# A mixture-of-experts decoder layer: two fixed units for the experts' outputs, and another look-ahead for the weights

## The chip, the cores and the metric

The kernel runs on one core of a Trainium2 chip. The metric is the device time of one execution in microseconds (us); the median of three runs is given, and beside it one execution that the hardware profiler recorded.

## The reference, cut to what matters

One decoder layer: a spatial gating MLP and a differential attention side by side, a cross-attention into 256 memory tokens, and a mixture of 32 experts, each token using two of them. The change lies in the experts:

```python
def hierarchical_moe(h, w_rg, b_rg, w_re, b_re, w_gate, w_up, w_down):
    ...                                  # routing: 1024 tokens, 2 experts each
    def expert_rows(args):               # xb: 128 rows of 1024, for one expert
        xb, e = args
        g = xb @ w_gate[e]               # 1024 x 512
        u = xb @ w_up[e]                 # 1024 x 512
        return (jax.nn.silu(g) * u) @ w_down[e]      # 512 x 1024
    y_rows = lax.map(expert_rows, (x_rows, block_expert)).reshape(P, D)
    ...
    out = jnp.einsum('nk,nkd->nd', wts.astype(y.dtype), y)
```

## The kernel before, in words

The last 600 us are the 32 experts, one after the other, each on one block of 128 rows. The input rows of an expert are gathered (POOL, an indirect DMA) into one of three buffers `xg`. `x_t` transposes them on TensorE (eight matmuls with the identity into the PSUM tile `px`) and splits them into a high part `xth` (a cast on ACT) and a low part `xtl` (a subtraction on DVE). `gate_up` multiplies by the gate and the up weights: 8 weight tiles, 48 matmuls of 128x512 into two PSUM tiles `pgu`, each product being three matmuls (high by high, high by low, low by high: `mm3`). ACT and DVE then form `hh` (DVE's step, L1424, ends it). `h_t` transposes `hh` (four matmuls into `pt`) and splits it into `ht`; `down` multiplies by 4 further weight tiles (24 matmuls into `py`). ACT scales `py` into a unit `y` in SBUF (L1450), and POOL issues a scatter that adds the rows of `y` to the tokens in DRAM (`x2d`, L1451). Each scatter waits for the landing of the one before.

`down(e-1)` is called after `gate_up(e)` and `x_t(e+1)`, and `h_t(e)` after that. The order of the instructions of POOL and SP is that of the code. The order of TensorE, ACT and DVE is that of the code for the first two experts and from the 31st on; between, a scheduler that works when the program is built puts it together, by what it believes is ready when. The order is then fixed: at run time each engine waits in that order.

Every weight tile (512 KB, `raw`) is loaded by SP, cast by ACT (`whi`, L280) and its rest formed by DVE (`wlo`, L281). `raw`, `whi`, `wlo`, `xth`, `xtl`, `ht` and `y` all take units of 128x1024 out of one pool of 45 (`unit`, tag "u"): a tile that is taken must wait until what last used its unit has let go of it. `pump` issues loads up to `ahead["load"]` tiles beyond the one in use: 31 tiles for experts 0 to 15, 10 from expert 16 on, 20 for the last. PSUM has one tag "pd" with two buffers for `px` and `py` alike, and one with four for `pgu` and `pt`.

After expert 30's scatter has landed, SP loads the 1024 tokens back (`xf`, eight loads, L1513), POOL gathers the rows of the last expert (L1515), and squares, norms, scaling and stores follow.

Of the kernel before, what the change touches and what calls it, by code (L numbers as in the profile page):

```python
# [19 lines left out]
D = 1024  # L20
KT = 8
H = 512
NE = 32
# [13 lines left out]
AL = 1  # L37
MD = 4.0
NX = 3
LA = 30  # L40
LE = 31
LD = 2
LS = 3
PF = 3
RM = {mybir.EngineType.DVE, mybir.EngineType.PE, mybir.EngineType.Activation}
PK = 12
LF = 10
EF = 16
JT = 0
ED = 1  # L50
KQ = lambda nc: nc.gpsimd
# [58 lines left out]
def tile_layer(tc, a, out):  # L110
# [12 lines left out]
    def unit(name, shape, dt=F32):  # L123
        return up.tile(shape, dt, name=name, tag="u", bufs=NU)
# [7 lines left out]
    def ps2(name="pd"):  # L132
        return psum.tile([128, 1024], F32, name=name, tag="pd", bufs=2)

    def mm3(o, sh, sl, mh, ml, start, stop):
        mm(o, sh, mh, start=start, stop=False)  # L136
        mm(o, sh, ml, start=False, stop=False)  # L137
        mm(o, sl, mh, start=False, stop=stop)  # L138
# [41 lines left out]
    def row(t, ap, n):  # L180
        nc.gpsimd.dma_start(t, bass.AP(tensor=ap.tensor, offset=ap.offset, ap=[[0, 128], [1, n]]))
# [81 lines left out]
    ahead = {"load": 3, "split": 1}  # L263
# [21 lines left out]
    def take():  # L285

        j = ptr["use"]
        ptr["use"] += 1
        pump()
        k = plan[j][1]  # L290
        return [t.rearrange("p (k c) -> p k c", k=k) for t in parts.pop(j)]
# [752 lines left out]
    def gather(e):  # L1044
        x = xg[e % NX]
        nc.gpsimd.indirect_dma_start(out=x, out_offset=None, in_=td[:, :],
                                     in_offset=bass.IndirectOffsetOnAxis(ap=idx[:, e:e + 1], axis=0),
                                     bounds_check=S - 1, oob_is_err=False)
# [333 lines left out]

    ahead["load"], ahead["split"] = LA, LS

    xts = {}
    def x_t(e):
        x = xg[e % NX]
        if e == 0:
            xh, xl = unit("xth", [128, D], F32R), unit("xtl", [128, D], F32R)
            for i in range(2):  # L1390
                p = ps1("px")
                cs = slice(512 * i, 512 * i + 512)
                for k in range(4):
                    nc.tensor.transpose(p[:, k * 128:(k + 1) * 128], x[:, (4 * i + k) * 128:(4 * i + k + 1) * 128],
                                        ident)
                split(xh[:, cs], xl[:, cs], p)
            xts[e] = (xh, xl)
            return
        px = ps2("px")
        for k in range(KT):  # L1400
            nc.tensor.transpose(px[:, k * 128:(k + 1) * 128], x[:, k * 128:(k + 1) * 128], ident)
        xh, xl = unit("xth", [128, D], F32R), unit("xtl", [128, D], F32R)
        split(xh, xl, px)
        xts[e] = (xh, xl)

    hts = {}

    def gate_up(e, between=None):
        xh, xl = xts.pop(e)
        gu = []  # L1410
        for w in range(2):
            p = ps1("pgu")
            for q in range(4):
                wh, wl = take()
                for k2 in range(2):
                    k = 2 * q + k2
                    ks = slice(k * 128, (k + 1) * 128)
                    mm3(p, xh[:, ks], xl[:, ks], wh[:, k2], wl[:, k2], k == 0, k == KT - 1)
            gu.append(p)
            if w == 0 and between:  # L1420
                between()
        hh = half("hh")
        nc.scalar.activation(hh, gu[0], AF.Silu, scale=tab[:, 1, e:e + 1])
        nc.vector.scalar_tensor_tensor(hh, gu[1], tab[:, 1, e:e + 1], hh, op0=OP.mult, op1=OP.mult)  # L1424
        hts[e] = hh

    def h_t(e):
        hh = hts[e]
        pt = ps1("pt")
        for k in range(4):  # L1430
            nc.tensor.transpose(pt[:, k * 128:(k + 1) * 128], hh[:, k * 128:(k + 1) * 128], ident)
        x = unit("ht", [128, 2, H], F32R)
        split(x[:, 0], x[:, 1], pt)
        hts[e] = x

    def down(e, between=None):
        x = hts.pop(e)
        py = ps2("py")
        for k in range(4):
            wh, wl = take()  # L1440
            ks = slice(k * 128, (k + 1) * 128)
            for c in range(2):
                cs = slice(c * 512, (c + 1) * 512)
                mm3(py[:, cs], x[:, 0, ks], x[:, 1, ks], wh[:, 0, cs], wl[:, 0, cs], k == 0, k == 3)
            if k == 1 and between:
                between()
        if e == NE - 1:
            return py
        y = unit("y", [128, D])
        nc.scalar.activation(y, py, AF.Copy, scale=tab[:, 0, e:e + 1])  # L1450
        nc.gpsimd.indirect_dma_start(out=x2d[:, :], out_offset=bass.IndirectOffsetOnAxis(ap=idx[:, e:e + 1], axis=0),  # L1451
                                     in_=y, in_offset=None, bounds_check=S - 1, oob_is_err=False,
                                     compute_op=OP.add)
# [11 lines left out]
    def count_blocks():  # L1465

        pc = ps1()
        for t in range(8):
            mm(pc[:, :NE], oneb, Mb[t // 4][:, 3 + t % 4], start=(t == 0), stop=(t == 7))
        nc.vector.tensor_scalar(nb, pc[:, :NE], 128.0, None, op0=OP.is_gt)  # L1470
        for j in range(2, 8):
            nc.vector.tensor_scalar(t1, pc[:, :NE], 128.0 * j, None, op0=OP.is_gt)
            nc.vector.tensor_add(nb, nb, t1)
        nc.vector.tensor_reduce(nov[:, 0:1], nb, axis=AX.X, op=OP.add)
        nc.vector.tensor_copy(novi, nov[:, 0:1])
    for e in range(NE):
        ahead["load"] = LF if e >= NE - EF else max(LE, LA - LD * e)
        gate_up(e, between=(lambda: h_t(0)) if e == 1 else None)
        if e + 1 < NE:
            x_t(e + 1)  # L1480
        if e + 1 + NX < NE:
            gather(e + 1 + NX)
        if e == NE - 2:
            last = tc.manual_schedule(engines=RM)
            last.__enter__()

            down(e - 1, between=lambda: h_t(NE - 2))
            break
        if e:
            down(e - 1)  # L1490
        if e:
            h_t(e)
        if e == 1:
            man.__exit__(None, None, None)
            count_blocks()
        if e == 4:
            with tc.manual_schedule(engines=RM):
                nr = nc.values_load(novi[0:1, 0:1], min_val=0, max_val=NOV - 1,
                                    skip_runtime_bounds_check_because="2048 assignments leave at most 15 further blocks")
        if e == PK:  # L1500
            gfin = unit("gfin", [128, D])
            row(gfin, a["norm_final"], D)


    e = NE - 1

    ahead["load"], ahead["split"] = 20, 5
    down(e - 1)
    st = op.tile([128, 2, 9], F32, name="rfin")
    xf = [unit("xf", [128, D]) for _ in range(8)]  # L1510
# [75 lines left out]
    with tc.If(nr > 0):  # L1586
# [63 lines left out]
        with tc.For_i(0, nr, 1) as b:  # L1650
# [41 lines left out]
            y = unit("oy", [128, D])  # L1692
# [51 lines left out]
def _build(arrays):  # L1744
    import numpy as np
    import concourse.bacc as bacc
    nc = bacc.Bacc("TRN2", target_bir_lowering=False, num_devices=1)
    a = {n[3:]: nc.dram_tensor(n, v.shape, mybir.dt.from_np(v.dtype), kind="ExternalInput").ap()
         for n, v in arrays.items()}
    out = nc.dram_tensor("out_0_dram", (S, D), mybir.dt.from_np(np.dtype("float32")), kind="ExternalOutput").ap()  # L1750
    with tile.TileContext(nc, schedule_with_timeline_sim=True) as tc:
        tile_layer(tc, a, out)
    return nc
# [8 lines left out]
```

## Time and profile before

| | |
|---|---|
| median of 3 runs | 1395.27 us (1391.04 to 1400.35) |
| the profiled execution | 1395.21 us |
| its span | 1393.3 us (1.9 us lie outside) |
| TensorE (PE) busy | 1321.9 us, 95% |
| VectorE (DVE) busy | 1002.0 us, 72% |
| ScalarE (ACT) busy | 836.1 us, 60% |

The span runs from the first instruction to the last. Of the busy share of TensorE one subtracts what the clock does to it: a matmul of 128x512 follows the one before after 0.23 us at full clock. Times below are counted from the span's start.

### The profile page before, as it was taken

The numbers are of one execution on the slowest core, as the hardware profiler recorded it, in microseconds if no ns is written. First come the engines' busy times: TensorE is split into PE (matmuls) and PEld (weight loads), VectorE is DVE, ScalarE is ACT, GpSimd is POOL, SyncE is SP. The second block draws the span as 40 slices with busy tenths as digits, with TensorE's granted clock in tenths as the row PEclk, the third lists the DMA queues.
The fourth block names the chain that finished last, engine by engine and source line by source line (L and its number), as shares of the span: only waits on it lengthen the run. The fifth ranks groups of instructions, "written<-read, shape, count | busy, mean of one in ns | idle before, by whom it ended". The sixth has DMA issues, their size and how long they took to land. (4 is left out here: it accounts for less than half of the span.)

```text
span 1393.3 us, 20524 instructions
## 1 busy us (share of the span) xinstructions
PE 1321.9 (95%) x7424; PEld 1145.1 (82%) x7424; DVE 1002.0 (72%) x1564; ACT 836.1 (60%) x1139; POOL 253.3 (18%) x284
## 2 busy tenths in 40 slices
PE   6999999999999999999998799999989999999992
PEld 4999998989887889999887688888778888888871
DVE  5787694677856444433455798999979999999985
ACT  6554553455555543333232588888868888888874
POOL 2421110311112321112112121111111111111010
PEclk9999999999999999999998899999999999999995
DMA  7640211311275664013699799999999699999986
GB/s 277 194 139 2 60 61 46 91 55 30 84 255 200 201 240 162 19 44 104 227 332 329 256 336 375 362 357 356 353 368 350 217 376 376 367 355 370 376 293 260
DMA packets 103225, 322.39 MB, mean 231 GB/s; under 512 B 15747, under 2 KB 23971, under 8 KB 103120
## 3 DMA queue, kind: packets, MB, share of 16 engines
q1 hardware_dynamic: 76896, 272.14, 53.2%
q0 software_dynamic: 17776, 40.51, 10.2%
q10 hardware_dynamic: 8448, 8.39, 1.8%
q8 instruction: 59, 0.97, 0.3%
q14 instruction: 46, 0.38, 0.1%
HBM read 287.10 MB, written 46.66 MB: 240 GB/s over the span
## 5 line engine op out<-in xcount | busy, mean ns | idle before, releaser
L281 DVE TENSOR_TENSOR wlo<-raw,whi 128x1024 fp32r<-128x1024 f32 (+1 forms) x469 | 557.3, 1227 | 76.4 <-ACT whi L280 68.8
L280 ACT CAST whi<-raw 128x1024 fp32r<-128x1024 f32 (+1 forms) x469 | 472.8, 1050 | 65.5 <-DVE wlo L281 10.8
L136 PE MATMUL pgu<-whi,xth 128*128 128x512 f32 x512 | 198.6, 396 | 4.4 <-ACT whi L280 3.3
L137 PE MATMUL pgu<-wlo,xth 128*128 128x512 f32 x512 | 201.1, 393 | 1.0 <-DVE wlo L281 1.0
L138 PE MATMUL pgu<-whi,xtl 128*128 128x512 f32 x512 | 200.4, 391 | 0.5 <-DVE xtl L142 0.5
L1451 POOL DMA_INDIRECT x2d<-y,idx x31 | 50.9, 1641 | 450.5 <-ACT y L1450 412.1
L136 PEld LDWEIGHTS pgu<-whi,xth 128*128 128x128 f32 x512 | 96.7, 189 | 26.0 <-ACT whi L280 5.2
L137 PEld LDWEIGHTS pgu<-wlo,xth 128*128 128x128 f32 x512 | 96.8, 189 | 22.8 <-DVE wlo L281 2.2
L138 PEld LDWEIGHTS pgu<-whi,xtl 128*128 128x128 f32 x512 | 96.7, 189 | 20.9 <-DVE xtl L142 1.2
L137 PE MATMUL py<-wlo,ht 128*128 128x512 f32 x256 | 104.0, 406 | 1.8 <-DVE wlo L281 1.8
L136 PE MATMUL py<-whi,ht 128*128 128x512 f32 x256 | 102.6, 401 | 0.7 <-ACT ht L141 0.7
L138 PE MATMUL py<-whi,ht 128*128 128x512 f32 x256 | 100.9, 394 | 0.0
L645 ACT ACTIVATE p<-p,stt 128x128 f32<-128x128 f32 (+7 forms) x64 | 49.7, 776 | 50.0 <-DVE stt L644 45.6
L137 PE MATMUL pp<-wlo,hTh 128*128 128x256 f32 x256 | 72.7, 284 | 1.3 <-DVE wlo L281 1.3
L136 PE MATMUL pp<-whi,hTh 128*128 128x256 f32 x256 | 73.1, 286 | 0.2 <-ACT whi L280 0.2
L136 PE MATMUL pp<-whi,h2h 128*128 128x256 f32 x256 | 73.1, 285 | 0.0
L137 PE MATMUL pp<-wlo,h2h 128*128 128x256 f32 x256 | 72.5, 283 | 0.0
L138 PE MATMUL pp<-whi,hTl 128*128 128x256 f32 x256 | 72.5, 283 | 0.0
L138 PE MATMUL pp<-whi,h2l 128*128 128x256 f32 x256 | 72.5, 283 | 0.0
L136 PE MATMUL pp<-hTh,whi 128*128 128x512 f32 x160 | 64.3, 402 | 0.4 <-ACT ot L697 0.4
L137 PE MATMUL pp<-hTl,whi 128*128 128x512 f32 x160 | 63.7, 398 | 0.0
L138 PE MATMUL pp<-hTh,wlo 128*128 128x512 f32 x160 | 63.4, 396 | 0.0
(365 smaller groups left out, 2941.2 us busy)
## 6 DMA issues: line engine op xcount, KB each, us to landing
raw<-in_w_gate SPq DMA_DIRECT2D x128, 512.0 KB, 10.6
raw<-in_w_up SPq DMA_DIRECT2D x128, 512.0 KB, 12.5
raw<-in_w_down SPq DMA_DIRECT2D x128, 512.0 KB, 11.2
raw<-in_w_in SPq DMA_DIRECT2D x19, 512.0 KB, 3.7
raw<-in_w_kv_mem SPq DMA_DIRECT2D x16, 512.0 KB, 5.9
raw<-vwd SPq DMA_DIRECT2D x16, 512.0 KB, 4.2
raw<-in_w_q_memT SPq DMA_DIRECT2D x8, 512.0 KB, 5.2
raw<-in_w_out SPq DMA_DIRECT2D x8, 512.0 KB, 5.3
```

Source lines behind the costliest of these rows:

```text
L136: mm(o, sh, mh, start=start, stop=False)
L137: mm(o, sh, ml, start=False, stop=False)
L138: mm(o, sl, mh, start=False, stop=stop)
L280: nc.scalar.copy(hi[:, c], raw[:, c])
L281: ahead.get("lo", nc.vector).tensor_tensor(lo[:, c], raw[:, c], hi[:, c].bitcast(F32), op=OP.subtract)
L645: nc.scalar.activation(pe[:, :nk], pe[:, :nk], AF.Exp, bias=stt[:, 2 + m:3 + m], scale=slopes[hd], accum_out=stt[:, 4 + m:5 + m])
L1451: nc.gpsimd.indirect_dma_start(out=x2d[:, :], out_offset=bass.IndirectOffsetOnAxis(ap=idx[:, e:e + 1], axis=0), in_=y, in_offset=None, bou ...
```

## The change

The outputs of the experts no longer take a unit of the pool each time. Two units are taken once, ahead of the loop, and expert e uses the unit `ys[e % 2]`. The look-ahead of the loads is 29 tiles up to expert 11 and 27 from expert 12 (`PK`) on; the numbers LD, LF and EF with which it fell to 10 from expert 16 are gone. The last expert keeps its 20.

```diff
-LA = 30
-LE = 31
-LD = 2
+LA = 29
+LE = 29
...
-LF = 10
-EF = 16
...
     hts = {}
+    ys = [unit("y", [128, D]) for _ in range(2)]
...
-        y = unit("y", [128, D])
+
+        y = ys[e % 2]
         nc.scalar.activation(y, py, AF.Copy, scale=tab[:, 0, e:e + 1])
...
     for e in range(NE):
-        ahead["load"] = LF if e >= NE - EF else max(LE, LA - LD * e)
+        ahead["load"] = LE if e < PK else LE - 2
```

The lines of the changed kernel stand two or three lower than before (`y` is L1449 there, `pt` L1429, `px` L1398, `whi` L277). Since the pool's units go round in another way, the scheduler finds other moments at which things are ready, and the order on TensorE, ACT and DVE differs from about expert 11 on. Three places follow. "waits X" names the engine or DMA queue whose semaphore the instruction waits for.

TensorE at expert 24, from the last matmuls of its `pgu` (which end ahead of the excerpt of before, 13 matmuls of `py` above its `pt`); before:

```order
L138 MATMUL py<-whi,ht 128x512
L136 MATMUL py<-whi,ht 128x512 [waits Activation_49]
L1431 MATMUL pt<-ident,hh 128x128 [waits DVE_49]
L1431 MATMUL pt<-ident,hh 128x128 x3
L137 MATMUL py<-wlo,ht 128x512 [waits DVE_49]
L138 MATMUL py<-whi,ht 128x512
L136 MATMUL py<-whi,ht 128x512
L137 MATMUL py<-wlo,ht 128x512
L138 MATMUL py<-whi,ht 128x512
L1401 MATMUL px<-ident,xg 128x128 [waits DMASW6_49,DVE_49]
L1401 MATMUL px<-ident,xg 128x128 x7
L136 MATMUL py<-whi,ht 128x512 [waits Activation_49]
```

And now:

```order
L133 MATMUL pgu<-whi,xth 128x512
L134 MATMUL pgu<-wlo,xth 128x512
L135 MATMUL pgu<-whi,xtl 128x512
L1429 MATMUL pt<-ident,hh 128x128 [waits DVE_49]
L1429 MATMUL pt<-ident,hh 128x128 x3
L1398 MATMUL px<-ident,xg 128x128 [waits DMASW4_49,Activation_49]
L1398 MATMUL px<-ident,xg 128x128 x7
L133 MATMUL py<-whi,ht 128x512 [waits DVE_49]
L134 MATMUL py<-wlo,ht 128x512
L135 MATMUL py<-whi,ht 128x512
```

The transposes `pt`, which wait for `hh` of the same expert, moved from among the matmuls of `py` to right behind the last matmul of `pgu`, `px` comes right behind them, and the first matmul of `py` now waits for DVE: for `xtl`, since `py` takes the PSUM buffer that `px` had.

DVE at the same expert, around `hh`; before:

```order
L281 TENSOR_TENSOR wlo<-raw,whi 128x1024 [waits DMAHW3_49,DVE_49,Activation_49]
L1424 SCALAR_TENSOR_TENSOR hh<-pgu,tab,hh 128x512 [waits PE_49]
L281 TENSOR_TENSOR wlo<-raw,whi 128x1024 [waits DMAHW4_49,DVE_49,Activation_49]
L142 TENSOR_TENSOR xtl<-px,xth 128x1024 [waits Activation_49]
L281 TENSOR_TENSOR wlo<-raw,whi 128x1024 [waits DMAHW5_49,Activation_49]
```

And now:

```order
L278 TENSOR_TENSOR wlo<-raw,whi 128x1024 [waits DMAHW4_49,PE_49,Activation_49]
L1422 SCALAR_TENSOR_TENSOR hh<-pgu,tab,hh 128x512 [waits PE_49]
L139 TENSOR_TENSOR xtl<-px,xth 128x1024 [waits DVE_49,Activation_49]
L278 TENSOR_TENSOR wlo<-raw,whi 128x1024 [waits DMAHW5_49,Activation_49]
L278 TENSOR_TENSOR wlo<-raw,whi 128x1024 [waits DMAHW6_49,DVE_49,Activation_49]
```

Here `xtl` stands next to `hh`, one `wlo` earlier than before.

ACT where the weights of expert 13 are cast; before:

```order
L1450 ACTIVATE y<-py,tab 128x1024 [waits PE_49]
L141 CAST ht<-pt 128x512 [waits DVE_49]
L280 CAST whi<-raw 128x1024 [waits DMAHW1_49,DVE_49]
L280 CAST whi<-raw 128x1024 [waits DMAHW2_49,PE_49]
L280 CAST whi<-raw 128x1024 [waits DMAHW3_49,DMASW0_49]
L280 CAST whi<-raw 128x1024 [waits DMAHW4_49,DMASW2_49,Activation_49]
L1423 ACTIVATE hh<-pgu,tab 128x512 [waits PE_49]
```

And now:

```order
L138 CAST ht<-pt 128x512 [waits DVE_49,PE_49]
L1449 ACTIVATE y<-py,tab 128x1024 [waits DMASW4_49]
L1449 ACTIVATE y<-py,tab 128x1024 [waits DMASW6_49,PE_49]
L277 CAST whi<-raw 128x1024 [waits DMAHW1_49,DVE_49]
L277 CAST whi<-raw 128x1024 [waits DMAHW2_49]
L277 CAST whi<-raw 128x1024 [waits DMAHW3_49,PE_49]
L277 CAST whi<-raw 128x1024 [waits DMAHW4_49,PE_49]
L277 CAST whi<-raw 128x1024 [waits DMAHW5_49,DVE_49]
```

The waits of the casts for POOL's queue of DMAs (DMASW, the scatters) are gone; in their place the writes of `y` wait for the scatter of two experts before, and two of them stand side by side here. The same happens at the end: the writes of `y` of experts 28 and 29 stand next to each other, where before sixteen other instructions lay between. Experts 25 and 29 have the same order as 24; at 26, 27 and 28 `px` comes right behind `pgu`, then `pt`, then `py`; at 30 `px`, then `py`. At 11, 22 and 23 `pt` comes right behind `pgu` and `py` behind it, whose first matmul waits for `xtl` too; at 12 it waits for `xtl` alone, which stands ahead of `hh` there. Experts 13 to 21 have no such wait behind `pgu`.

## Rows read from the trace of the kernel before

**Rows 1.** The page: busy time, share of the span, instructions.

```profile
PE   1321.9 (95%) x7424; PEld 1145.1 (82%) x7424; DVE 1002.0 (72%) x1564; ACT 836.1 (60%) x1139; POOL 253.3 (18%) x284
```

**Rows 2.** Windows: length, busy PE, PEld, DVE, ACT, POOL, clock, DMA share, GB/s.

```profile
1074.00:1098.00 24.00, 24.00 (x114) 19.96 (x113) 22.34 (x21) 20.81 (x24) 5.50 (x4) 1.00 0.43 136
1098.00:1250.00 152.00, 152.00 (x726) 126.68 (x725) 140.67 (x130) 124.34 (x137) 23.95 (x16) 1.00 1.00 368
1250.00:1340.00 90.00, 89.66 (x420) 73.74 (x419) 83.18 (x77) 75.75 (x83) 11.95 (x8) 1.00 1.01 372
```

**Rows 3.** Timeline of POOL, experts 11 to 14: start, duration, instruction, idle before.

```profile
1011.84 1.58 POOL L1451 DMA_INDIRECT x2d<-y,idx  x1 [14.47 <-DMA raw<-in_w_down]
...
1037.05 1.61 POOL L1451 DMA_INDIRECT x2d<-y,idx  x1 [21.63 <-ACT y L1450]
...
1055.90 1.60 POOL L1451 DMA_INDIRECT x2d<-y,idx  x1 [15.55 <-ACT y L1450]
...
1073.66 1.58 POOL L1451 DMA_INDIRECT x2d<-y,idx  x1 [14.43 <-ACT y L1450]
```

**Rows 4.** Timeline of ACT, the late cast.

```profile
1020.70 1.04 ACT L280 CAST whi<-raw 128x1024 fp32r<-128x1024 f32 x1 [4.34 <-issue]
```

**Rows 5.** Timeline of PE, the same place.

```profile
1021.80 0.54 PE L136 MATMUL pgu<-whi,xth 128*128 128x512 f32 x1 [2.16 <-ACT whi L280]
```

**Rows 6.** Window behind it, same columns as rows 2.

```profile
1022.20:1028.90 6.70, 5.98 (x15) 4.60 (x15) 5.05 (x5) 4.85 (x6) 0.00 (x0) 0.50 0.90 349
```

**Rows 7.** Waits of ACT, 1250 to 1350: total, times, longest.

```profile
ACT whi L280 <- DMA raw<-in_w_down: 7.9, 7, 2.2
```

**Rows 8.** Timeline of PE in an expert without waits.

```profile
1153.29 0.39 PE L138 MATMUL pgu<-whi,xtl 128*128 128x512 f32 x1
...
1156.24 0.60 PE L1431 MATMUL pt<-ident,hh 128*128 128x128 f32 x4
1156.59 0.48 PE L137 MATMUL py<-wlo,ht 128*128 128x512 f32 x1
...
1158.07 1.04 PE L1401 MATMUL px<-ident,xg 128*128 128x128 f32 x8
1158.86 0.48 PE L137 MATMUL py<-wlo,ht 128*128 128x512 f32 x1
```

**Rows 9.** Timeline of DVE, the same expert.

```profile
1153.71 0.75 DVE L1424 SCALAR_TENSOR_TENSOR hh<-pgu,tab,hh 128x512 f32<-128x512 f32 x1 [0.27 <-PE pgu L138]
1154.38 1.22 DVE L281 TENSOR_TENSOR wlo<-raw,whi 128x1024 fp32r<-128x1024 f32 x1
```

**Rows 10.** Timeline of all engines, end of expert 0, where `px` follows `pgu`.

```profile
790.12 0.39 PE L138 MATMUL pgu<-whi,xtl 128*128 128x512 f32 x1
...
790.35 1.03 PE L1401 MATMUL px<-ident,xg 128*128 128x128 f32 x8
...
791.42 1.01 ACT L141 CAST xth<-px 128x1024 fp32r<-128x1024 f32 x1 [0.54 <-PE px L1401]
...
792.47 1.23 DVE L142 TENSOR_TENSOR xtl<-px,xth 128x1024 fp32r<-128x1024 f32 x1 [0.80 <-ACT xth L141]
...
793.75 0.50 PE L138 MATMUL pgu<-whi,xtl 128*128 128x512 f32 x1 [0.53 <-DVE xtl L142]
```

**Rows 11.** Timeline of all engines, last scatter and last expert.

```profile
1350.60 2.48 POOL L1451 DMA_INDIRECT x2d<-y,idx  x1 [9.54 <-ACT whi L280]
...
1356.64 0.75 DVE L1424 SCALAR_TENSOR_TENSOR hh<-pgu,tab,hh 128x512 f32<-128x512 f32 x1
...
1357.44 1.12 PE L1431 MATMUL pt<-ident,hh 128*128 128x128 f32 x4 [2.88 <-DVE hh L1424]
1358.12 2.61 SPq L1513 DMA_DIRECT2D xf<-x2d  x5
...
1359.82 0.63 PE L137 MATMUL py<-wlo,ht 128*128 128x512 f32 x1
```

**Rows 12.** Timeline of PE, the last matmul of `pgu` of expert 30.

```profile
1330.54 0.39 PE L138 MATMUL pgu<-whi,xtl 128*128 128x512 f32 x1
```

## The prediction

> **What bounds the kernel now.** I start with the page: TensorE is busy for 95% of the span [rows 1], so I look for what stops it, stage by stage, and then for what the change puts in its way. The windows of the expert stage come next. From 1098 to 1250 TensorE has no idle time at all (152.00 of 152.00), at full clock [rows 2]. DVE is busy for 140.67 of those 152 us, 93%, and the DMA engines for all of it [rows 2]. TensorE sets the pace, but DVE and the DMA have little to give: a few microseconds lost on TensorE can't be won back later, since its matmuls already follow each other at their own pitch (0.23 us, from the last `pgu` at 790.12 to `px` at 790.35 [rows 10]).
>
> The timeline of POOL shows the pace and the one hole in it. The scatters start at 1011.84, 1037.05, 1055.90 and 1073.66 [rows 3]: 25.2, 18.85, 17.8. The regular period is 17.7. So 25.2 + 18.85 − 35.4 = 8.65 us are lost at expert 13. The timeline of ACT names the cause: a weight cast starts at 1020.70 after 4.34 us of idling put down to "issue" [rows 4], and the order of ACT has this cast wait for a scatter's queue. The scatter issued at 1011.84 lands 8.9 us later, at 1020.7. The cast's unit was the `y` that this scatter still read. TensorE stands for 2.16 us [rows 5] and then runs at a granted clock of 0.50, the 1.2 GHz level, for 6.7 us [rows 6], which costs half of that, 3.35; the rest are shorter gaps around it.
>
> The loads are the second thing that could bound. The look-ahead falls from 31 tiles to 10 at expert 16, and from 1074 to 1098 the DMA idles more than half of the time, 0.43 [rows 2]. After that it works without a break and still, from 1250 to 1350, casts wait for a load of `down` seven times, 7.9 us [rows 7]. TensorE feels little of that: 0.34 of 90 us [rows 2], and about 0.5 as its share of the last scatters' spacing.
>
> **The change, part by part.** *The `y` units.* No weight tile takes over a unit that a scatter reads, so the waits at expert 13 go: −8.65 us. What takes their place is the wait of `y` itself for the scatter of two experts before; 35.4 us lie between, against a landing of 8.9, so it costs nothing where the writes of `y` keep their spacing.
>
> *The look-ahead.* 27 instead of 10 over the second half: there is no pause of the loads. The pause cost 24 us at (1 − 0.43), 13.7 us of DMA time. Against it stand four tiles less than 31 (2.1 MB at 368 GB/s, 5.7 us). The loads of the second half come about 8 us earlier, and the 0.5 us of starved casts go: −0.5.
>
> *The order.* This is the largest term. Behind the last matmul of `pgu` (start S) TensorE used to have 13 matmuls of `py` that needed nothing new, and `pt` came 2.95 us later, at 1156.24 after 1153.29 [rows 8], when `hh` was long done. In ten experts, and at expert 30, the new order puts there something that has yet to be made. The steps from rows: `hh` starts at S + 0.42 (1153.71) and DVE takes the next at S + 1.09 (1154.38) [rows 9]; from the start of `hh` to `pt` 0.80 (1356.64 to 1357.44 [rows 11]); `pt` occupies TensorE for 0.35, `px` for 0.79 [rows 8]; from the start of `px` over `xth` and `xtl` to the matmul that waits for `xtl` 3.40 (790.35 to 793.75), and from the start of `xtl` alone 1.28 (792.47 to 793.75) [rows 10]. Then:
> - Experts 24, 25 and 29 (`pt`, `px`, `py`): `pt` at S + 0.42 + 0.80 = S + 1.22, `px` at S + 1.57, `py` at S + 1.57 + 3.40 = S + 4.97. Without a wait `py` would start at S + 0.23 + 0.35 + 0.79 = S + 1.37. Loss 3.6 each, 10.8.
> - Experts 26, 27 and 28 (`px`, `pt`, `py`): `px` at S + 0.23, `py` at S + 3.63, `pt` lies in between. Loss 3.63 − 1.37 = 2.26 each, 6.8.
> - Expert 23 (`pt`, `py` behind an `xtl` that follows `hh`): `xtl` at S + 1.09, `py` at S + 2.37, against S + 0.58. Loss 1.8. At 11 and 22 the order is the same, but the `wlo` ahead of `hh` may start late, as its unit comes free only with the last tiles; I add 0.85 and 0.65 of at most one `wlo` (1.13 by pitch) as estimates: 2.65 and 2.45. At 12 `xtl` stands ahead of `hh` behind a `wlo` of the same sort, an estimate of 0.9. Together 7.8.
> Sum 25.4 us. What could hide them is `py` not being tied to `px`: it takes the PSUM buffer that `px` of the next expert has just used, and with another it could start at once. In the built order the wait on DVE is there. Bounds: 0 if `xtl` is early for a reason that I don't see; 31 if half of the ten find one more `wlo` of DVE (1.13) in the way.
>
> *Expert 30 and the tail.* `px` and then `py` behind `pgu`: 3.63 − 0.23 − 0.79 = 2.6 on TensorE. On POOL more is lost. The writes of `y` of experts 28 and 29 now stand side by side, late, and that of 27 not far ahead, near the end of expert 30's `pgu`; so four scatters follow, each behind the other's landing. The last scatter of before took 7.5 us until the loads of `xf` (1350.60 to 1358.12 [rows 11]), with few loads beside it. Four times that from S + 1.5 put the `xf` loads at S + 31.5, instead of 1358.12 − 1330.54 [rows 12] = 27.6 or, since at S the new order has some four matmuls fewer behind it, 26.7. I take 5 us, the 2.6 of TensorE lying beside them. Bounds: 2.6, if the writes come earlier; 17, if each of the three spacings is like the one before the last scatter (9.54 of idling [rows 11] and the 1.9 of the scatter ahead, 11.4; 3 × 3.9 more).
>
> *The clock.* Each stall of 2.16 us [rows 5] and of 2.88 us [rows 11] was followed by matmuls at half clock (0.63 a matmul [rows 11] in place of 0.39 [rows 8]); no shorter one in the expert stage was. Seven of the new idle stretches come near, by the steps above and with `pt` and `px` breaking up the longer waits: 3.40 − 0.79 less the transposes that still run, about 2.4, at 24, 25, 29 and 30, and about 2 at 26 to 28. I take one and a half falls at 3.35 us, 5 us; bounds 0 and seven falls, 23.
>
> The Trainium skill, "TensorE: Matmul & The Clock Gate", section "Loop structure matters more than you think", has the clock fall with long waits for DMA and not with a copy by DVE out of PSUM between groups; the new waits are for such a copy. By it the clock term would be 0 and the time 1416.5. Rows 11 speak against it: the 2.88 us there were a wait for DVE, and half clock followed.
>
> Sum against the profiled execution of 1395.2, the same as the median within 0.1: 1395.2 − 8.65 − 0.5 + 25.4 + 5 + 5 = **1421.5 us**. I say 1421.
>
> **The rivals.**
> - *The new waits are hidden; only the gain is left.* The mechanism is that `xtl` and `hh` of the next experts are ready before TensorE asks, because DVE, which was delayed at expert 13 before, runs ahead. It decides from the point at which `xtl` of an expert is done before S + 1.4. For it: DVE idles 7% in rows 2, and experts 13 to 21 have no such wait. Against it: `hh` needs the last `pgu`, which no engine can bring forward, and `px` stands behind `pgu` on TensorE's own queue. Time: 1395.2 − 8.65 − 0.5 = 1386, and 1381 if the tail gains what it was forecast to lose. Not slower, and mostly within 1%.
> - *The clock doesn't fall* (the rule above): 1416.5.
> - *The clock falls at each of the seven and the scatters land late*: four falls instead of one and a half are 8.4 more, 1430; all seven and 5 more in the tail 1444.
> - *The loads starve TensorE.* Twelve loads and a gather and a scatter, 14 × 0.524 MB, take 17.1 us (the loads alone at 368 GB/s) to 19.9 an expert against 17.7. Over seven experts at most 2.2 each: 15, so 1386 + 15 = 1401, if the new waits were hidden. With the new waits TensorE is slower than the loads and nothing is added. Against it: the loads come 8 us earlier than before.
>
> **How the numbers follow.** The forecast with a clock loss of 2 to 8 us (1418 to 1425, and wider by its order term) 0.50; without a clock loss 0.20; clock and scatters high 0.12; waits hidden 0.15; starved with waits hidden 0.03. The likeliest is 1421. The range leaves out the hidden waits (0.18 with the starved ones) and little above: its low end is 1403, about half of the new waits and of the tail (1395.2 − 9.15 + 15.2 = 1401) and no clock loss; its high end is 1434, the forecast with the order's upper bound (+6) and two more falls of the clock (+6.7). Within 1% is about what a measurement of this kernel can tell from no change. Faster by over 1% (below 1381.3): 0.05, a third of the hidden waits. Within 1%: 0.17, the rest of them, the starved case and 0.04 of waits half hidden. Slower by over 1% (above 1409.2): 0.78.
>
> **What the changed profile would show.** Right: scatters at even spacing around expert 13 and no cast with 4.3 us of "issue"; idle time on PE <-DVE `xtl` and `hh` of some 3.6 us an expert at 24, 25 and 29, and 2.3 at 26 to 28, with scatter spacings of about 20 to 21 us there; four scatters in a row some 7.5 to 9 us apart ahead of the `xf` loads; DMA with no pause, but below its full share at the end. Wrong: spacings of 17.7 throughout (the first rival), casts idle for loads (the fourth), or a window of experts 24 to 29 with the clock at 1.00 (the second). The forecast fails most easily if `xtl` runs earlier than `px` by way of a buffer swap that I misread, or by the clock.

## The result, and the profile after

The changed kernel takes 1419.34 us (median of 4 runs, 1414.86 to 1423.43) against 1396.24 of the kernel before (4 runs): a ratio of 1.0162, 95% interval 1.0144 to 1.018. It is slower by 23.1 us. The profiled execution was the slowest of its four, 1423.43 us with a span of 1421.7, so the two profiles differ by 28.4 us. The runs differ in the clock alone, as far as they show: span times mean clock is 1379.0 in the profiled one (1421.7 × 0.970) and 1380.6 in the fastest (1413.1 × 0.977).

The page of the changed kernel, busy time, share and instructions:

```profile
PE   1328.6 (93%) x7424; PEld 1150.1 (81%) x7424; DVE 1000.7 (70%) x1564; ACT 839.9 (59%) x1139; POOL 264.2 (19%) x284
```

TensorE's work is the same (7424 matmuls, as in [rows 1]); its share fell by two points. Where it waits stands in the waits of PE of the changed kernel from 975 to 1375 (engine, line, waited for: us in total, times, longest):

```profile
PE py L133 <- DVE xtl L139: 15.6, 11, 2.4
PE pt L1429 <- DVE hh L1422: 7.8, 8, 1.7
PE py L133 <- ACT y L1449: 0.8, 1, 0.8
```

These are the waits that the prediction read off the built order, eleven of `py` for `xtl` and eight of `pt` for `hh`. The kernel before has neither at experts 11 to 30. The timeline of PE at expert 24, and behind it at 25, shows how they lie (start, duration, instruction, idle before):

```profile
1222.88 0.66 PE L1429 MATMUL pt<-ident,hh 128*128 128x128 f32 x4 [0.85 <-DVE hh L1422]
...
1226.77 0.50 PE L133 MATMUL py<-whi,ht 128*128 128x512 f32 x1 [2.36 <-DVE xtl L139]
```

```profile
1244.27 0.66 PE L1429 MATMUL pt<-ident,hh 128*128 128x128 f32 x4 [0.85 <-DVE hh L1422]
1244.76 1.04 PE L1398 MATMUL px<-ident,xg 128*128 128x128 f32 x8
1248.16 0.50 PE L133 MATMUL py<-whi,ht 128*128 128x512 f32 x1 [2.36 <-DVE xtl L139]
...
1249.65 0.62 PE L133 MATMUL py<-whi,ht 128*128 128x512 f32 x1
```

From the start of `px` (1244.76) to the matmul of `py` (1248.16) 3.40 us pass, to the hundredth what [rows 10] had at the end of expert 0. At 1249.65 the matmul takes 0.62: the clock has fallen. It falls after five of the eight waits of experts 23 to 30, and not after those of 11, 12 and 22. The windows behind the waits of 24 (no fall), 25, 26, 27 (none), 28, 29 and 30, columns as in rows 2 (the clock is the third number from the end):

```profile
1226.70:1231.00 4.30, 4.23 (x18) 3.49 (x19) 3.65 (x5) 2.76 (x4) 0.00 (x0) 1.00 1.03 343
...
1248.00:1254.00 6.00, 5.84 (x19) 4.67 (x20) 4.17 (x5) 2.87 (x4) 0.00 (x0) 0.72 1.02 376
...
1269.60:1276.00 6.40, 6.35 (x21) 5.07 (x22) 4.08 (x4) 3.21 (x4) 0.00 (x0) 0.73 1.02 371
1291.00:1298.00 7.00, 6.89 (x30) 5.73 (x31) 5.76 (x7) 4.69 (x6) 0.00 (x0) 1.00 1.03 390
1310.90:1318.00 7.10, 7.03 (x24) 5.66 (x25) 5.04 (x6) 4.26 (x5) 0.00 (x0) 0.76 0.99 332
1333.90:1341.00 7.10, 7.09 (x24) 5.66 (x25) 5.23 (x5) 4.22 (x5) 0.00 (x0) 0.76 0.66 185
1355.40:1360.00 4.60, 4.60 (x14) 3.67 (x15) 2.21 (x2) 0.58 (x1) 0.00 (x0) 0.63 0.11 21
```

Length times (1 − clock) is the time lost: 6.0 × 0.28 = 1.68, then 1.73, 1.70, 1.70 and 1.70, 8.5 us in all. The clock itself is at half for about 3.4 us each time.

The tail, from the timelines of POOL and SP, the last four scatters and the loads of `xf`:

```profile
1350.85 1.60 POOL L1450 DMA_INDIRECT x2d<-y,idx  x1 [20.63 <-ACT y L1449]
1364.24 1.59 POOL L1450 DMA_INDIRECT x2d<-y,idx  x1 [11.79 <-ACT y L1449]
1370.98 2.16 POOL L1450 DMA_INDIRECT x2d<-y,idx  x1 [5.15 <-ACT whi L277]
1378.75 2.34 POOL L1450 DMA_INDIRECT x2d<-y,idx  x1 [5.61 <-DMA x2d<-y,idx]
```

```profile
1385.60 4.80 SPq L1512 DMA_DIRECT2D xf<-x2d  x8
```

The last three scatters stand 6.7 and 7.8 us apart and the loads come 6.9 behind; in [rows 11] it was 7.5. The first of the four stands 13.4 us ahead of the second, which waited for the write of its `y`.

Where the 28.4 us are shows in the start of the last matmul of `pgu` of each expert (S of the prediction), taken from the timelines of PE, with the distance from one to the next. The regular distance is 17.69.

| expert | before | its step | after | its step | after − before |
|---|---|---|---|---|---|
| 0 | 790.12 | | 792.10 | | +1.98 |
| 10 | 966.41 | 17.69 | 967.16 | 17.69 | +0.75 |
| 11 | 984.71 | 18.29 | 984.62 | 17.46 | −0.09 |
| 12 | 1003.04 | 18.33 | 1005.06 | 20.44 | +2.02 |
| 13 | 1027.92 | 24.88 | 1023.84 | 18.78 | −4.08 |
| 15 | 1064.85 | 18.74 | 1059.40 | 17.66 | −5.45 |
| 22 | 1188.43 | 17.69 | 1182.82 | 17.69 | −5.61 |
| 23 | 1206.12 | 17.69 | 1202.97 | 20.15 | −3.15 |
| 24 | 1223.81 | 17.69 | 1221.64 | 18.67 | −2.17 |
| 25 | 1241.49 | 17.69 | 1243.04 | 21.39 | +1.55 |
| 26 | 1259.18 | 17.69 | 1266.02 | 22.99 | +6.84 |
| 27 | 1276.87 | 17.69 | 1287.48 | 21.46 | +10.61 |
| 28 | 1294.55 | 17.69 | 1307.34 | 19.86 | +12.79 |
| 29 | 1312.85 | 18.30 | 1328.78 | 21.44 | +15.93 |
| 30 | 1330.54 | 17.69 | 1351.77 | 22.99 | +21.23 |
| 31 | 1354.15 | 23.62 | 1380.25 | 28.48 | +26.10 |
| end of span | 1393.3 | | 1421.7 | | +28.4 |

The loss at expert 13 is gone, 3.8 us come in at 12 and 13 (the stalls behind 11 and 12), nothing happens until 22, and from there every expert costs 1 to 5 us more. The step to 24 is the shortest of these because its matmuls have no `px` among them (0.79 us of work in [rows 8]); that `px` stands in the step from 30 to 31, where the kernel before has none.

### The profile page after: what moved, and what is told of

Same layout as the page of the kernel before. It is cut to its first block, busy times and chain, and to the rows that moved or that the text cites. A ratio compares the mean times of both kernels' runs of the same rounds, so it can differ in the third digit from the quotient of the medians.

```text
span 1421.7 us, 20488 instructions
## 1 busy us (share of the span) xinstructions
PE 1328.6 (93%) x7424; PEld 1150.1 (81%) x7424; DVE 1000.7 (70%) x1564; ACT 839.9 (59%) x1139; POOL 264.2 (19%) x284
## 5 line engine op out<-in xcount | busy, mean ns | idle before, releaser
L277 ACT CAST whi<-raw 128x1024 fp32r<-128x1024 f32 (+1 forms) x469 | 474.0, 1049 | 75.2 <-PE py L134 19.7
L133 PE MATMUL py<-whi,ht 128*128 128x512 f32 x256 | 105.5, 412 | 17.1 <-DVE xtl L139 15.6
L135 PE MATMUL py<-whi,ht 128*128 128x512 f32 x256 | 103.0, 402 | 0.0
L133 PEld LDWEIGHTS py<-whi,ht 128*128 128x128 f32 x256 | 49.9, 195 | 30.8 <-DVE xtl L139 17.6
L1043 POOL DMA_INDIRECT xg<-td,idx x32 | 54.0, 1689 | 53.8 <-DVE wsel L1167 17.6
```

The lines of the kernel that those rows point to most:

```text
L277: nc.scalar.copy(hi[:, c], raw[:, c])
```

## The experiments

Two theories stood against each other and a third beside them. A: the time lies in what TensorE finds behind `pgu`, by the order that the scheduler builds. B: the shorter look-ahead costs by itself, through loads that come late. C: the wait of `y` for its scatter costs by itself. All ratios are against the kernel before, run on the same chip.

**The units alone.**

```diff
 # the kernel before, look-ahead 31 and 10 kept
+    ys = [unit("y", [128, D]) for _ in range(2)]
...
-        y = unit("y", [128, D])
+        y = ys[e % 2]
```

> The kernel before with the two fixed units for y alone; the look-ahead stays 31 tiles, and 10 from expert 16 on. Theory A (the loss is the order behind pgu, which only the two parts of the change together bring): the built order has pt among the matmuls of py at every expert and no py that waits for xtl, and no cast waits for a scatter any more, so only the gain is left: 1395 - 9 to 10 = 1386 us, faster than before; no idle stretch of PE over 1 us in the experts, no half clock there. Rival B (the shorter look-ahead itself costs): 1386 too. Rival C (the wait of y for the scatter of two experts before holds ACT up): 1405 to 1420.

1412.92 us, ratio 1.0124 (1.0096 to 1.0152): a miss for A as it was put. In the built order of TensorE `pt` indeed stays among the matmuls of `py`, 7 or more of them behind `pgu` at every expert from 2 on, and no wait of `py` for `xtl` is there. But the order of ACT moved: the write of `y` now stands ahead of casts that the next `pgu` needs, and ACT stands still until the last matmul of `py` is done. Waits of ACT from 1180 to 1320, and one of them in the timeline:

```profile
ACT y L1451 <- PE py L138: 27.9, 7, 4.1
```

```profile
1253.84 1.12 ACT L1451 ACTIVATE y<-py,tab 128x1024 f32<-128x1024 f32 x1 [4.08 <-PE py L138]
```

The casts behind it come late, and each of experts 21 to 28 takes 18.6 to 18.9 us, each of 4 to 16 (but 13) 18.2 to 18.6, where before took 17.7. A further 8.5 us went behind the last expert; there POOL shows one scatter of 16.14 us (below). So the units bring a bad order even without the look-ahead, on another engine. The number lies in the range of C, but C is not shown by it: what holds ACT up is `py`, not a scatter.

**The look-ahead alone.**

```diff
 # the kernel before, y out of the pool
-LA = 30
-LE = 31
+LA = 29
+LE = 29
...
-        ahead["load"] = LF if e >= NE - EF else max(LE, LA - LD * e)
+        ahead["load"] = LE if e < PK else LE - 2
```

> The kernel before with the look-ahead of the change alone (29, and 27 from expert 12 on); y still takes a unit of the pool each time. Theory A: the built order keeps pt well behind pgu, py waits for no xtl; casts still take over units that scatters read, so a stall like that of expert 13 may remain at another place or go: 1386 (none) to 1398 (one like it). Rival B: as slow as the changed kernel less its gain at expert 13, 1415 to 1428, with idle casts waiting for loads. Rival C: as A.

1396.24 us, ratio 1.0008 (0.9993 to 1.0022): no change, within A's range and against B. The stall at expert 13 shrank (step 19.13 instead of 24.88; no cast of "issue" stands there), and S of expert 15 came 7.5 us earlier than before. Of this 1.5 us were left at S of expert 31: the experts from 24 on had steps of up to 19.5. The waits of PE from 1180 to 1350 say why:

```profile
PE pt L1431 <- DVE hh L1424: 6.8, 5, 1.5
```

A's expectation of the order failed here. At experts 24, 25, 27, 28 and 29 `pt` and `px` stand right behind `pgu` in this built order too, as at 24, 25 and 29 of the changed kernel, and `pt` waits for `hh`; but `py` starts behind `px` without a wait. No cast of ACT waits for a load in this stretch.

**px and py each in a PSUM buffer of its own.**

```diff
 # the changed kernel
-    def ps2(name="pd"):
-        return psum.tile([128, 1024], F32, name=name, tag="pd", bufs=2)
+    def ps2(name="pd", own=None):
...
+        return psum.tile([128, 1024], F32, name=name, tag=f"pd{turn[0] % 2 if own is None else own}", bufs=1)
...
-        px = ps2("px")
+        px = ps2("px", 0)
...
-        py = ps2("py")
+        py = ps2("py", 1)
```

> The changed kernel, with px and py each in a PSUM buffer of its own in place of two shared ones. Then py waits for the write of the y before instead of for xtl of the expert after next in line. Theory A: the 15.6 us of py waiting for xtl go (15.6 and their starts, some 18), and with them most of the falls of the clock (8); the waits of pt for hh (8.8 us) stay or grow, and py may wait for y, at most about 1 us an expert: 1395 to 1408. Rival B (look-ahead): no change, 1419. Rival C: 1419 or more, since py now hangs on y directly.

1432.95 us, ratio 1.0255 (1.0226 to 1.0285), a miss: the waits of `py` for `xtl` are gone, but the scheduler answered with yet another order. A cast waits on ACT for 4.86 us for a unit that TensorE's `pgu` still holds, and experts 13, 23 and 24 take 29.1, 27.6 and 29.5 us. The number lies in the range of C, but `py` waits for `y` for only 0.9 us between 1180 and 1350. An edit that the scheduler may answer doesn't isolate a wait; hence the runs by hand.

**Three units in turn.**

```diff
 # the changed kernel
-    ys = [unit("y", [128, D]) for _ in range(2)]
+    ys = [unit("y", [128, D]) for _ in range(3)]
...
-        y = ys[e % 2]
+        y = ys[e % 3]
```

> The changed kernel with three units for y in turn in place of two. The built order is that of before up to expert 21 and, from 22 on, has the rest of py right behind pgu, then pt; no py waits for xtl. Theory A: pt has five matmuls of py ahead of it, 1.1 us, about what hh needs (1.2), so 0.1 to 0.5 us an expert are lost over eight experts: 1386 to 1393. Rival B: 1415 or more (the look-ahead is that of the change). Rival C: partly better than the change, 1400 to 1415.

1395.77 us, ratio 0.9996 (0.9981 to 1.0011): with the look-ahead of the change, and no tie of `py` to `xtl`, the 23 us are gone. That speaks against B. It is 3 us above A's range, though: at expert 23 the kernel is 9 us ahead of before, and by 29 it has lost nearly all of that. It is the wait that A names, but longer. PE from 1180 to 1350:

```profile
PE pt L1429 <- DVE hh L1422: 8.0, 5, 2.3
```

At experts 24, 25, 27, 28 and 29 `pt` comes right behind `pgu`, and not behind five matmuls of `py` as A had it; one fall of the clock, at expert 25, adds 6.00 × 0.28 = 1.7 (1234 to 1240, clock 0.72). Casts wait for loads for 3.2 us in all from 1190 to 1340.

**The order by hand.** To take the scheduler out, the order of TensorE, DVE and ACT was written for experts 2 to 29:

```diff
 # the changed kernel
     for e in range(NE):
+        if e == 2:
+            hand = tc.manual_schedule(engines=RM)
+            hand.__enter__()
+            x_t(3)
+            gather(3 + NX)
         gate_up(e, between=(lambda: h_t(0)) if e == 1 else None)
...
+            down(e - 1, between={1: h, 2: xt})    # behind the 2nd tile: h_t(e); behind the 3rd: x_t(e + 2) and its gather
```

> The changed kernel (two units for y, look-ahead 29 and 27) with the order of TensorE, DVE and ACT written out for experts 2 to 29, as the scheduler had it before: pgu, 12 matmuls of py, pt, 6 of py, px of the expert after next, 6 of py; casts three tiles ahead. Theory A (order): the two parts of the change cost nothing by themselves, 17.7 us an expert, no stall at expert 13: 1380 to 1388. Rival B and C together (fewer tiles ahead, or y waiting for its scatter, cost by themselves): 1405 to 1420. A third: three tiles ahead are too few for casts by hand, every expert some 0.5 us longer, 1395 to 1400.

1390.40 us, ratio 0.9961 (0.9947 to 0.9975): the fastest kernel of the study, with both parts of the change in it. By the order alone it stands 2.0% under the changed kernel (0.9961 against 1.0162). That settles A against B and C: with this order neither part of the change costs what they say. The size was off by 2 us at the least; experts 4 to 12 took 18.07 us. Late in the stage TensorE waits for hardly anything, 0.6 us from 1180 to 1350.

> The kernel before (y out of the pool, look-ahead 31 and 10) with the same order by hand. Theory A: differs from the run by hand with the two units only in what the units and the look-ahead do: casts wait for scatters where they take over the unit of a y that was just written, 0 to 10 us in all: 1383 to 1398. Rivals B and C: faster than that run by 20 or more.

1416.90 us, ratio 1.0156 (1.0138 to 1.0174), a miss by 19 us. It has the same order with the units and the look-ahead of before. Two things differ from the run above, so a further run took them apart:

> The order by hand and the look-ahead of the change, 29 and 27, but y out of the pool. It differs from the run by hand in the units of y alone, and from the run by hand with 31 and 10 in the look-ahead alone. If the 26 us between those two are the look-ahead of 31, which leaves the casts too few units: 1388 to 1394. If they are units that scatters hold: 1410 to 1417.

1397.57 us, ratio 1.0003 (0.9991 to 1.0016), between the two ranges and nearer the first. So, in this order, the look-ahead is worth 1.0156 − 1.0003 = 1.5% and the units 0.4%. What the look-ahead of 31 does is in the waits of ACT of the run with 31 and 10, from 980 to 1090:

```profile
ACT whi L280 <- PE pgu L137: 17.0, 27, 1.3
```

31 loaded tiles of 45 units leave the casts so few that they wait for units which TensorE is just done with; experts 9 to 15 take 19.0 to 22.2 us, and those from 17 to 25, where 10 are ahead, 17.69. What the pool does to `y` is in one row of DVE of the run with 29 and 27 out of the pool:

```profile
824.30 1.23 DVE L281 TENSOR_TENSOR wlo<-raw,whi 128x1024 fp32r<-128x1024 f32 x1 [5.07 <-issue]
```

It looks like [rows 4] at another expert, the second, and on DVE: a tile that takes over the unit of a `y` whose scatter hasn't landed. The view names no releaser; the scatter was issued at 814.29, 10.0 us before, and in [rows 4] the cast started 8.9 behind the issue. TensorE stands 4.58 us, and that step is 6.5 us longer than in the run by hand.

**The tie, made by hand.**

```diff
 # the run by hand, from expert 22 to 29
-            down(e - 1, between={1: h, 2: xt})
+            tie[0] = e % 2          # px and py of this turn in the same buffer; None in the other run
+            h()
+            xt()
+            down(e - 1)
...
```

Up to expert 21, and where `tie` is None, `px` and `py` have a PSUM buffer each in both runs.

> As the run by hand, but from expert 22 to 29 pt and px stand right behind pgu and py behind them, in the PSUM buffer that px of the same turn used, as at experts 24, 25 and 29 of the changed kernel. Theory A: 3.6 us for each of eight experts, 28.8, and a fall of the clock for more than half of them at 1.7: 34 to 42 more than the run by hand. Rival (the order of pt alone, not the tie of py to px): 8 to 10 more.

> As the tied run, same order, but px and py each keep a PSUM buffer of their own, so that py waits for nothing of px. Theory A: only hh is missing behind pgu, pt at S + 1.22 instead of S + 0.23, 1.0 us for each of eight experts: 8 more than the run by hand, with no or few falls of the clock. Rival (the place of pt and px costs, not the tie): as the tied run.

Tied 1443.07 us (ratio 1.0346, 1.0317 to 1.0375), free 1409.25 (1.009, 1.0068 to 1.0111). The tie alone is worth 33.8 us in eight experts, 4.2 each. They lie 53 and 19 us above the run by hand, where A gave 34 to 42 and 8; the waits of PE say why. Tied, from 1190 to 1390:

```profile
PE py L137 <- DVE xtl L143: 18.9, 8, 2.4
PE pt L1433 <- DVE hh L1426: 15.2, 7, 3.4
```

Free, from 1190 to 1350:

```profile
PE pt L1433 <- DVE hh L1426: 15.2, 7, 3.4
```

The wait for `xtl` is 2.36 us in each of the eight, and in the free run it is gone while the order is the same: it is the tie, not the place of `px`. The wait for `hh` is 1.7 to 3.4 us here, mostly 2.1, and 0.63 to 0.85 at experts 23 to 29 of the changed kernel, because by hand the `wlo` of the casts stand ahead of `hh` on DVE. At expert 24 of the free run, whose `pgu` has its last matmul at 1230.49:

```profile
1222.75 9.51 DVE L282 TENSOR_TENSOR wlo<-raw,whi 128x1024 fp32r<-128x1024 f32 x8 [0.72 <-ACT whi L281]
1232.17 0.74 DVE L1426 SCALAR_TENSOR_TENSOR hh<-pgu,tab,hh 128x512 f32<-128x512 f32 x1
```

And the clock, in the windows from S of expert 22 to S of expert 30, tied and free:

```profile
1184.43:1385.89 201.46, 165.35 (x675) 131.91 (x673) 135.95 (x122) 125.47 (x132) 17.81 (x13) 0.86 0.83 290
```

```profile
1184.83:1351.72 166.89, 149.66 (x674) 122.42 (x673) 134.83 (x122) 124.90 (x132) 17.81 (x13) 0.96 0.96 351
```

The tied run takes 34.6 us more there. TensorE idles 36.1 us of its window and 17.2 of the free one's: 18.9 of the difference are the wait for `xtl` itself. The other 15.7 are busy time, the same work at a lower clock. So a little under half of what the tie costs comes by way of the clock.

**Fewer tiles ahead.** Three runs with 25 or 22 tiles:

```diff
-LE = 29
+LE = 25                  # 22 in the second run; LE in place of LE - 2 from expert 12 on
```

> The run by hand with a look-ahead of 25 tiles in all experts but the last, in place of 29 and 27. Theory (units, not loads, bind there: with 29 ahead an expert took 18.07 us, with 27 17.7 to 17.8): 17.69 from the fourth expert on, 0.38 for ten experts and 0.1 for ten more saved, 4 to 5 us less than the run by hand: 1384 to 1387. Rival (fewer loads ahead starve the casts at the end): 1390 or more, with casts idle for loads after 1250.

> The run by hand with a look-ahead of 22 tiles. Theory: the units no longer bind, so no gain over 25, 1384 to 1387; or the loads come short at the end, up to three tiles at 1.4 us: up to 4 us more, with casts idle for loads after 1250.

> The changed kernel, order by the scheduler, with a look-ahead of 25 tiles in all experts but the last. Its built order ties py to xtl at eleven experts, as that of the changed kernel does. Theory A (the order sets it): 1412 to 1428, idle PE <-DVE xtl of 12 us or more. Rival B (the look-ahead sets it): as the run by hand with 25, under 1390.

By hand with 25: 1393.71 us, 0.9977 (0.9966 to 0.9988); with 22: 1394.89, 0.9992 (0.998 to 1.0004). The changed kernel with 25: 1414.86, 1.0126 (1.011 to 1.0142), with waits of `py` for `xtl` at nine experts (12 and 23 to 30, 18.0 us), which once more puts the order above the look-ahead. The runs by hand did what the theory said up to expert 19, 17.69 each, so with 29 ahead it was the units that held them; then they didn't keep it, and both lie above the theory's ranges, the run with 25 in its rival's. With 25 tiles S of expert 22 is 8.1 us earlier than before; experts 23 to 28 take 18.9 to 19.6 each, and S of expert 31 is 1352.32, beside 1352.34 with 29 and 27, 1352.30 with 22, 1354.15 in the kernel before, and 1354.01 with three units. Waits of ACT of the run with 25, from 1200 to 1290, and its window:

```profile
ACT whi L277 <- DMA raw<-in_w_down: 13.2, 10, 2.6
```

```profile
1200.00:1290.00 90.00, 84.64 (x398) 68.87 (x397) 77.46 (x72) 72.16 (x78) 14.74 (x9) 1.00 0.99 368
```

The casts wait for loads and the DMA engines are full; `hh` on DVE comes later by it, and `pt` on TensorE waits some 1.0 us an expert. This is shown for the runs by hand with 25 and 22 alone. The look-ahead alone and the three units lost their gain to `pt` behind `pgu`, and the run by hand with 29 and 27 lost most of it before expert 22. That S of expert 31 agrees so closely has no one cause, as far as these rows show.

## Why the prediction was right

The forecast was 1421 us, the median 1419.3, the profiled execution 1423.4. By its own steps:

- *The stall at expert 13.* Forecast −8.65. The steps of 11 to 15 exceed 17.69 by 9.98 before, by 3.79 after. The gain was 10.0; the scatters' spacing, from which it was read, leaves out 0.5 to 1.1 us at each of the neighbours. The rows by which it would show are there: no cast of "issue" waits.
- *The order.* The steps of the changed kernel less 17.69, and less 1.7 where the clock fell, are the stalls behind each expert: 11: 2.75 (forecast 2.65), 12: 1.09 (0.9), 22: 2.46 (2.45), 23: 1.77 (1.8; its step has no `px`, so it is taken less 16.90), 24: 3.70 (3.6), 25: 3.62 (3.6), 26: 2.04, 27: 2.17 and 28: 2.05 (2.26 each), 29: 3.60 (3.6). Sum 25.2, forecast 25.4. None is off by more than 0.25; those of 11, 12 and 22 had an estimate in them.
- *Expert 30 and the tail.* Behind 30: 28.48 − 23.62 − 1.70 = 3.2 (forecast 2.6; 0.8 of it is the `px` that the step to 24 lacks, and `py` also waits 0.8 for the `y` that stands late). From S of expert 31 to the end 2.3 more than before. Together 5.5, forecast 5. The way to it was another, so that it came near is in part luck: the prediction had four scatters 7.5 apart from S + 1.5 and the loads of `xf` at S + 31.5; there were three in a row, from S + 12.5, and the loads came at S + 33.8, of which 1.7 are the clock.
- *The clock.* Forecast 5 as one and a half falls at 3.35. It was five falls at 1.7, 8.5. Both factors were wrong, and that the sum came near is luck; this is the mis-sized term. What made the factors wrong: the stall of [rows 5] was followed by 6.7 us at half clock [rows 6], these by about 3.4, and a fall came already after idling of 1.73, and of 0.64 and 1.07 with `pt` between (at expert 26), while the same 0.63 and 1.07 at expert 27 and 2.36 at expert 24 had none. The 8.5 are those of the profiled run, the slowest of its four. From the spans and mean clocks of the others, length times (1 − clock) is 42.7 us in the profiled run and 38.3, 39.7 and 32.5 in the others, so by an estimate (8.5 less the difference to 42.7, good to about 1.5 us) the middle two lost some 4 to 6 us to new falls and the fastest (1414.86 us) nothing. That the clock doesn't fall, a rival at 1416.5, is what the fastest run looks like; it was not profiled. The Trainium skill ("TensorE: Matmul & The Clock Gate", section "Loop structure matters more than you think") has a copy by DVE out of PSUM leave the clock up, in a loop whose next matmuls follow at once. Here they don't: all five falls of this trace stand behind a wait for `xtl`, a subtraction by DVE out of PSUM, of 1.07 to 2.36 us, so the rule could not be carried over to the new waits.
- *The look-ahead.* Forecast −0.5, and TensorE never starved in the changed kernel, since it was slower than the loads: its casts wait for a load once between 975 and 1375, for 0.2 us. That holds. But the first rival's price, 1386, was reached by no run without the tie. With the new waits taken away by hand the kernel came to 1390.4, held by the units up to expert 12; with three units to 1395.8, and with the look-ahead alone to 1396.2, held by `pt` right behind `pgu`. The fourth rival, loads that starve TensorE, was put at up to 1401 and at a chance of 0.03; it came with fewer tiles ahead than the change has (25 and 22, by hand), at 1393.7 and 1394.9. Its upper price for the loads of an expert, 19.9 us, took full rows for gather and scatter; the steps there are 18.9.

Terms and sum, against the profiles: +0.75 up to expert 10, −10.0, +3.8, −0.2 in drift up to 22, +31.7 from 22 to 31 (the 0.6 that before lost at 29 among it, and 8.5 of clock), +2.3 behind: 28.4.

Which part of the change made the scheduler tie `py` to `px` was not forecast. The runs say that it takes both. With the shorter look-ahead `pt` or `px` comes right behind `pgu` at every expert from 24 to 30 in each of the orders that the scheduler built for the shared PSUM tag: the look-ahead alone, two units, three units, and two units with 25 tiles. The tie came only where there were two units besides. Two units with 31 and 10 have neither; they have the bad order of ACT. What in the scheduler's reckoning makes the difference was not tried.

## What to carry to other kernels

Where a scheduler fixes the order when the program is built, an edit to a buffer is an edit to the order of every engine: read the built order behind each place where an engine runs out of independent work, and price what it waits for from the nearest rows of the old trace; ten stalls were foreseen to within 0.25 us in this way. An edit that the scheduler may answer is no experiment on a wait; write the order by hand and change one thing in it. And before a stall is booked as a gain, look at what else is full: in the run by hand with 25 tiles, with the DMA at 0.99, 8 us won at expert 22 came to 2 at expert 31.

## What the runs showed of the hardware

- The clock of TensorE fell to half after idling as short as 1.07 us (with 0.64 ahead of it), and not after the same at the next expert, nor after 2.36 at another; each of the five falls lasted about 3.4 us. In a kernel with eight such waits in a row (the tied run) the mean clock over 201 us was 0.86.
- In the profiled run with the units alone, one scatter held POOL for 16.14 us, where others take 1.6. The DMA share was 0.12 meanwhile, as the last weight load had been issued at 1343.8. Timeline of POOL:

```profile
1348.42 16.14 POOL L1452 DMA_INDIRECT x2d<-y,idx  x1 [17.04 <-ACT y L1451]
1369.45 1.55 POOL L1452 DMA_INDIRECT x2d<-y,idx  x1 [4.90 <-DMA x2d<-y,idx]
```

The loads of `xf` wait behind it, and the tail is 8.5 us longer than before. What held it was not found.
- Half a megabyte a load, with gathers and scatters between them, came to 368 GB/s on this core with the DMA at 0.99 (the run by hand with 25 tiles, 1200 to 1290); most experts there took 18.9 us for their twelve tiles, a gather and a scatter.
